# RWKV-7 recurrence: two 128-column products per chunk and head in place of four of 64 columns, y and its group norm by tokens

## The chip, the cores and the metric

The kernel runs on one core of a Trainium2 chip. The metric is the device time of one execution in microseconds (us), as the median of several runs. The profile is one execution taken by the hardware profiler; its times are counted from the first instruction.

## The reference, cut to what matters

The program is a two-layer encoder trunk over 512 tokens and 2048 channels: an RWKV-7 layer, then differential attention, each with a post-norm. The change is in the first layer, which has 32 heads of 64 channels. Each head keeps a 64 x 64 state:

```
def step(S, inp):                     # per token, all heads
    r_t, w_t, k_t, v_t, kk_t, a_t = inp
    sa = S @ kk_t
    S = S * w_t - outer(sa, kk_t * a_t) + outer(v_t, k_t)
    y = S @ r_t
...
mu, var = mean(y), var(y)             # per head and token
y = (y - mu) * rsqrt(var + GN_EPS) * gn_g + gn_b
y = y + sum(r * k * r_k) * v          # the bonus
out = (y * silu(g)) @ w_out
```

## The kernel before, in words

**Dense products.** Every projection is a run of 16 products, each with 16 k-tiles. For a k-tile, `step` issues three 128x512 matmuls into the tile `mm` (operands are split in a high and a low part). After each k-tile `fill.tick()` lets every pending job, a Python generator, issue its next piece; a job's `yield n` makes it sit out n ticks. Matmuls and DMAs keep the order in which the program issues them, on TensorE and on the queue of SP. The other engines' instructions are ordered by a scheduler, and those under `tc.high_priority()` go early.

**The recurrence by chunks.** Tokens are cut in 8 chunks of 64 (`NCH`, `L`), heads are taken in 16 pairs, a pair to 128 partitions. While the value projection runs (and the first gate products), these jobs share the ticks:

- `phase2(p)` prepares pair p: products of the keys `bdK` with `AR` (128 columns, two per tick), the centred values by tokens (`cen`, products of 64 columns into either half of the partitions, 16 instructions per tick), transposes of `bdK` (four per tick), products of the inverses `bdX` with `R`. The results are kept in `LAR`, `W` and `Q` (`qs` in the profile). It takes some 12 ticks of the 16 that a pair has.
- `chain(p)` runs the recurrence of pair p, two ticks per chunk. In the first tick one product per head, `LAR` with the state in `W`, gives u (tile `u`), which ScalarE copies into `W` (L829, L830). In the second tick one product per head, `Q` with `W`, gives the new state, which VectorE scales, adds to `nl` and writes to `W` (L844), for all chunks but the last; then two products per head add y in the tile `y`, one bank for the pair. All of these have 64 weight columns: head 0 writes partitions 0 to 63, head 1 partitions 64 to 127.
- `post(p)` makes the group norm with channels on partitions: squares, two 128x512 products with ones (`onesr`) for the sums, an inverse root by Newton steps on 128x512 tiles, gain and bonus, then one DMA to `d_y`.
- `solve` and `join` make the triangular inverses of a group of four pairs on GpSimd, with small products (64 weight columns) by `join`.

An F32 product is two instructions in the trace (a weight load and a matmul each), a transpose or an F32R product one: 30 products `u` of a pair are 60 instructions, its 32 products `y` are 64.

**Around it.** `load_r`, `load_k`, `load_ar` and `load_x` bring a pair's data from DRAM on SP's queue, `gates()` loads `d_y` later, multiplies it by the gate and splits it for the output projection. The inputs `xin` of the next projection are loaded by GpSimd's queue and mixed by ScalarE and GpSimd. Between these jobs there is no other order than the ticks.

## Time and profile before

| what | value |
|---|---|
| median of 3 runs | 2375.23 us (2374.12 to 2375.89) |
| span of the profiled execution | 2371.4 us |
| its own time beside the span | not given by the page; the median lies 3.8 us above the span |
| TensorE busy | 2281.1 us, 96% of the span |
| VectorE, ScalarE, GpSimd busy | 1371.7, 1085.0, 598.1 us |
| mean granted TensorE clock | 0.983 |

The span is from the first to the last instruction; the runs are timed from outside. Busy times are sums over an engine's instructions, and as matmuls overlap, a busy TensorE is not one at its peak: how long it takes for a piece of work is read from the starts.

### The profile page before, as it was taken

The page shows a single profiled execution, that of the slowest core. Times are in us where ns is not written, and L with a number is a line of the kernel's source. Part 1 is how long each engine was busy: PE and PEld are TensorE (multiplying, and loading weights), DVE is VectorE, ACT ScalarE, POOL GpSimd, SP SyncE. Part 2 cuts the span into 40 slices and gives each one's busy share as a digit, 9 for nine tenths or more (in the row PEclk, how much of TensorE's full clock was granted, in tenths as well). Part 3 has the DMA queues.
Part 4 walks back from the last instruction along what each step waited for, and adds up shares of the span by engine and source line. Part 5 has one row for each costly group of instructions (what it writes and reads, how often), then busy time and mean ns, then how long its engine had stood idle before and what let it go on. Part 6 is the DMA issues. An engine that isn't in the chain of part 4 may idle for free.

```text
span 2371.4 us, 34536 instructions
## 1 busy us (share of the span) xinstructions
PE 2281.1 (96%) x12894; PEld 1822.3 (77%) x12894; DVE 1371.7 (58%) x2451; ACT 1085.0 (46%) x2228; POOL 598.1 (25%) x817
## 2 busy tenths in 40 slices
PE   8999999989999999999999989999999999999995
PEld 5887877777667776678888768888888888888884
DVE  7556887795566666764445465353453544536554
ACT  6556655564555556643333353343333433334223
POOL 4223052858563335720023240000000000000113
PEclk9999999989999999999999999999999999999997
DMA  6445555577546545533333312222222222222222
GB/s 213 143 136 178 169 190 177 170 222 213 135 126 162 150 132 146 153 102 135 116 107 120 116 62 89 89 80 89 89 81 96 80 91 81 89 89 80 98 90 88
DMA packets 195079, 294.93 MB, mean 124 GB/s; under 512 B 115296, under 2 KB 119648, under 8 KB 194912
## 3 DMA queue, kind: packets, MB, share of 16 engines
q10 hardware_dynamic: 45648, 166.22, 20.8%
q1 hardware_dynamic: 144144, 109.71, 16.3%
q0 software_dynamic: 5120, 16.81, 2.5%
q8 instruction: 101, 1.65, 0.3%
q14 instruction: 66, 0.54, 0.1%
HBM read 239.13 MB, written 45.15 MB: 120 GB/s over the span
## 4 chain that ended last, share of the span: by engine, by line
PE 79%; POOL 7%; DVE 4%; issue 3%; DMA 3%; ACT 2%; SPq 1%; POOLq 0%; ACTq 0%; DVEq 0%
PE mm L105 64%; PE big L105 6%; PE u L105 2%; POOL z L605 2%; POOL tm L603 2%; DMA xin<-in_xT 2%; PE s L105 1%; PE y L105 1%; PE o L105 1%; PE big L108 1%; POOL xm L269 1%; SPq L111 1%; PE t L108 1%; POOL xin L268 1%; DVE wlo L176 1%
## 5 line engine op out<-in xcount | busy, mean ns | idle before, releaser
L105 PE MATMUL mm<-xh,whi 128*128 128x512 f32 x2560 | 1043.6, 408 | 6.7 <-ACT xh L231 2.3
L105 PE MATMUL mm<-xl,whi 128*128 128x512 f32 x2560 | 1006.7, 393 | 11.5 <-DVE xl L232 6.6
L105 PE MATMUL mm<-xh,wlo 128*128 128x512 f32 x2560 | 1006.3, 393 | 5.7 <-DVE wlo L176 5.5
L176 DVE TENSOR_TENSOR wlo<-wraw,whi 128x512 fp32r<-128x512 f32 x640 | 474.5, 742 | 597.7 <-ACT whi L175 564.3
L175 ACT CAST whi<-wraw 128x512 fp32r<-128x512 f32 x640 | 396.9, 620 | 727.3 <-PE mm L105 712.7
L105 PEld LDWEIGHTS mm<-xh,wlo 128*128 128x128 f32 x2560 | 483.9, 189 | 112.3 <-DVE wlo L176 8.5
L105 PEld LDWEIGHTS mm<-xl,whi 128*128 128x128 f32 x2560 | 485.4, 190 | 105.2 <-DVE xl L232 10.6
L105 PEld LDWEIGHTS mm<-xh,whi 128*128 128x128 f32 x2560 | 484.7, 189 | 104.6 <-ACT xh L287 4.9
L1118 POOL TENSOR_SCALAR dist<-dist 128x512 f32<-128x512 f32 x8 | 12.4, 1546 | 654.6 <-DVE zz L1148 654.6
L836 POOL TENSOR_SCALAR nl<-W,gls 64x64 f32<-64x64 f32 x224 | 115.0, 513 | 158.6 <-DVE W L844 146.3
L844 DVE SCALAR_TENSOR_TENSOR W<-u,gls,nl 64x64 f32<-64x64 f32 x224 | 63.4, 283 | 91.8 <-PE u L105 70.5
L266 ACT ACTIVATE xm<-xin,omu 128x512 f32<-128x512 f32 x96 | 68.2, 721 | 46.3 <-DMA xin<-in_xT 36.8
L603 POOL TENSOR_TENSOR tm<-z,at 128x31 f32<-128x31 f32 (+15 forms) x124 | 81.1, 654 | 31.1 <-DMA at<-d_ad 22.8
L605 POOL TENSOR_TENSOR z<-z,tm 128x31 f32<-128x31 f32 (+15 forms) x124 | 85.9, 693 | 8.4
L969 POOL TENSOR_TENSOR lna<-lna,zt 128x512 f32<-128x512 f32 x26 | 42.6, 1639 | 170.0 <-DVE zt L1244 115.8
L268 POOL TENSOR_SCALAR xin<-xin,vec 128x512 f32<-128x512 f32 x54 | 48.7, 902 | 140.6 <-ACT xm L266 52.1
L269 POOL TENSOR_TENSOR xm<-xm,xin 128x512 f32<-128x512 f32 x54 | 81.8, 1517 | 3.5
L829 ACT COPY W<-u 64x64 f32<-64x64 f32 x128 | 26.3, 205 | 101.6 <-PE u L105 94.7
L105 PEld LDWEIGHTS u<-W,LAR 128*64 128x64 f32 x512 | 28.7, 135 | 55.5 <-DVE W L844 27.3
L1077 POOL TENSOR_TENSOR xin<-xin,lns 128x512 f32<-128x512 f32 x15 | 19.7, 1311 | 194.6 <-ACT lns L957 148.9
L1147 ACT ACTIVATE sc<-sc,mx 128x128 f32<-128x128 f32 (+3 forms) x64 | 35.9, 561 | 57.8 <-DVE mx L1145 57.8
L288 DVE TENSOR_TENSOR xl<-xm,xh 128x512 fp32r<-128x512 f32 x64 | 57.4, 909 | 6.4 <-ACT xh L287 5.6
(246 smaller groups left out, 2742.2 us busy)
## 6 DMA issues: line engine op xcount, KB each, us to landing
wraw<-in_w_in ACTq DMA_DIRECT2D x125, 512.0 KB, 3.7
wraw<-in_w_oa ACTq DMA_DIRECT2D x32, 512.0 KB, 3.6
wraw<-in_w_v ACTq DMA_DIRECT2D x32, 512.0 KB, 3.5
wraw<-in_w_k ACTq DMA_DIRECT2D x32, 512.0 KB, 3.4
wraw<-in_w_q ACTq DMA_DIRECT2D x32, 512.0 KB, 3.5
wraw<-in_w_g ACTq DMA_DIRECT2D x32, 512.0 KB, 3.5
wraw<-in_w_ob ACTq DMA_DIRECT2D x32, 512.0 KB, 3.5
xin<-in_xT POOLq DMA_DIRECT2D x48, 256.5 KB, 3.8
```

The lines of the kernel that those rows point to most:

```text
L105: tc.keep_in_program_order(nc.tensor.matmul(*args, **kw))
L108: tc.keep_in_program_order(nc.tensor.transpose(*args))
L175: S.copy(hi, raw)
L176: V.tensor_sub(lo, raw, hi.bitcast(F32))
L266: S.mul(t, xt[:, 1:T + 1], sc)
L268: G.tensor_scalar(xp, xp, mu, 0.0, ALU.mult, ALU.add)
L269: G.tensor_add(t, t, xp)
L288: V.tensor_sub(lo, raw, hi.bitcast(F32))
L603: G.tensor_tensor(tv, z[:, j:j + 1, 0:n].broadcast_to([P, ni, n]), at_[:, j, j + 1:H2].rearrange("p (i o) -> p i o", o=1).broadcast_to([P, ...
L605: G.tensor_tensor(z[:, j + 1:H2, 0:n], z[:, j + 1:H2, 0:n], tv, ALU.subtract)
L836: G.tensor_scalar(nl[r], W[r, h, c, 0], gl[r], 0.0, ALU.mult, ALU.add)
L844: V.scalar_tensor_tensor(W[r, h, c + 1, 0], pm_[r, 0:L], gl[r], nl[r], ALU.mult, ALU.add)
```

## The change

In `chain`, the weights of a product become the whole of `LAR[:, h, c]` (128 columns: the 64 for u and the 64 for y) and of `Q[:, h, c]` (64 for the state, 64 for y), and the moving operand stays a block of 64 columns of `W`. So each chunk and head has two products with 128 weight columns, and y comes out by tokens, in two parts in the half that u and the state do not use. ScalarE copies u and the first part of y together, VectorE adds the second part once per two chunks. The last chunk, too, has its product with `Q`. One PSUM tile holds two chunks; the bank of `y` goes to a third `u` buffer.

`post` works with tokens on partitions: the sum of squares is a reduction along the free axis, the inverse root is made on 128x8 values, then four transposes bring y back to channels. Four DMAs with runs of 256 bytes store `d_y`. Gain and bonus move to `gates()`; for this the bonus is stored in `d_b` by `phase2` and loaded again. `AR` is kept by chunks, and `LAR` is loaded by three DMAs, two with runs of 256 bytes. Comments are taken out, so lines move; the diff is cut to what works differently.

```diff
-    d_ar = dtiles("d_ar", [P, 2, T])
+    d_ar = dtiles("d_ar", [P, NCH, 2, L])
...
-        LAR = p2.tile([P, 2, 2, NCH, L], F32, tag="LAR", name="LAR")
-        W = p2.tile([P, 2, NCH, 2, L], F32, tag="W", name="W")
-        for h, r in HEADS:
-            dma(LAR[r, h], AR[r].rearrange("p w (c t) -> p w c t", t=L))
+        LAR = p2.tile([P, 2, NCH, 2, L], F32, tag="LAR", name="LAR")
+        W = p2.tile([P, NCH, 5, L], F32, tag="W", name="W")
+        dma(LAR[lo_, 0], AR[lo_])
+        for w in range(2):
+            dma(LAR[hi_, 1, :, 1 - w], AR[hi_, :, w])
...
-            S.mul(Q[hi_, 1, cq], pxv[hi_], -1.0)
+            S.mul(Q[hi_, 1, cq, L:P], pxv[hi_, :, 0:L], -1.0)
+            S.mul(Q[hi_, 1, cq, 0:L], pxv[hi_, :, L:P], -1.0)
...
-        bv = p2.tile([P, T], F32, tag="bv", name="bv")
+        bv = p2.tile([P, T], F32, tag="bv", name="bv", bufs=1)
         V.tensor_mul(bv, vt, st["bz"])
...
+        dma(d_b[p], bv)
...
     def chain(p):
...
         for c in range(NCH):
-            pu = ps_u.tile([P, T], F32, tag="u", name="u")
+            cc = c % 2
+            if cc == 0:
+                pc = ps_u.tile([P, T], F32, tag="u", name="u").rearrange("p (c k h t) -> p c k h t", k=2, h=2, t=L)
             for h, r in HEADS:
-                mm(pu[r, 0:L], lhsT=LAR[:, h, 0, c], rhs=W[:, h, c, 0], start=True, stop=True)
+                mm(pc[:, cc, 0, h], lhsT=LAR[:, h, c].rearrange("p w t -> p (w t)"), rhs=W[:, c, 4 * h], start=True, stop=True)
             with tc.high_priority():
-                S.copy(W[lo_, 0, c, 1], pu[lo_, 0:L])
-                S.copy(W[hi_, 1, c, 1], pu[hi_, 0:L])
+                for h, r in HEADS:
+                    S.copy(W[r, c, 1 + h:3 + h], pc[r, cc, 0])
...
             yield 1
+            for h, r in HEADS:
+                mm(pc[:, cc, 1, h], lhsT=Q[:, h, c], rhs=W[:, c, 1 + 2 * h], start=True, stop=True)
             if c + 1 < NCH:
-                pm_ = ps_u.tile([P, T], F32, tag="u", name="u")
-                for h, r in HEADS:
-                    mm(pm_[r, 0:L], lhsT=Q[:, h, c, 0:L], rhs=W[:, h, c, 1], start=True, stop=True)
                 with tc.high_priority():
                     for h, r in HEADS:
-                        V.scalar_tensor_tensor(W[r, h, c + 1, 0], pm_[r, 0:L], gl[r], nl[r], ALU.mult, ALU.add)
-            for h, r in HEADS:
-                mm(py[r, cs], lhsT=W[:, h, c, 0], rhs=LAR[:, h, 1, c], start=True, stop=False)
-                mm(py[r, cs], lhsT=W[:, h, c, 1], rhs=Q[:, h, c, L:P], start=False, stop=True)
+                        V.scalar_tensor_tensor(W[r, c + 1, 4 * h], pc[r, cc, 1, h], gl[r], nl[r], ALU.mult, ALU.add)
+            if cc:
+                for h, r in ((0, hi_), (1, lo_)):
+                    V.tensor_add(ys[r, c - 1:c + 1], W[r, c - 1:c + 1, 2], pc[r, :, 1, h])
             yield 1
-        ys = p2.tile([P, T], F32, tag="ys", name="ys", bufs=1)
-        S.copy(ys, py)
...
     def post(p):
-        hi = p2.tile([P, T], F32R, tag="ngy", name="hi", bufs=1)
-        lo = p2.tile([P, T], F32R, tag="ngu", name="lo", bufs=1)
-        S.copy(hi, y2)
-        V.tensor_sub(lo, y2, hi.bitcast(F32))
-        yield 3
-        pv = big()
-        mm(pv, lhsT=onesr, rhs=hi, start=True, stop=False)
-        mm(pv, lhsT=onesr, rhs=lo, start=False, stop=True)
-        V.tensor_scalar(y2, pv, 1.0 / L, GN_EPS, ALU.mult, ALU.add)
-        rs = rsqrt(y2, p2, [P, T], "ng", 1, True)
-        V.scalar_tensor_tensor(ys, ys, RS_C, rs, ALU.mult, ALU.mult)
-        V.scalar_tensor_tensor(bv, ys, vcol("gg", p), bv, ALU.mult, ALU.add)
-        yield 10
-        dma(d_y[p], bv)
+        S.activation(y2, ys, AF.Square)
+        ss = p2.tile([P, NCH], F32, tag="ss", name="ss")
+        V.tensor_reduce(ss, y2, axis=AX.X, op=ALU.add)
+        V.tensor_scalar(ss, ss, 1.0 / L, GN_EPS, ALU.mult, ALU.add)
+        rs = rsqrt(ss, p2, [P, NCH], "ng")
+        V.tensor_mul(ys, ys, rs.rearrange("p (c o) -> p c o", o=1).broadcast_to([P, NCH, L]))
+        yield 9
+        pt = big()
+        for i in range(4):
+            transpose(pt[:, i * P:(i + 1) * P], ys[:, 2 * i:2 * i + 2].rearrange("p c v -> p (c v)"), ident)
+        yt = p2.tile([P, 4, 2, L], F32, tag="yt", name="yt", bufs=1)
+        S.copy(yt, pt.rearrange("p (i h t) -> p i h t", h=2, t=L))
+        yield 2
+        for cc, r in HEADS:
+            for h in range(2):
+                dst = d_y[p][h * L:(h + 1) * L].rearrange("v (i c t) -> v i c t", c=2, t=L)
+                dma(dst[:, :, cc], yt[r, :, 1 - h])
...
     def gates():
...
             dma(y, d_y[p])
+            dma(bb, d_b[p])
             yield 6
+            V.scalar_tensor_tensor(y, y, der[:, 4, p:p + 1], bb, ALU.mult, ALU.add)
             V.scalar_tensor_tensor(y, y, vcol("gb", p), th, ALU.add, ALU.mult)
```

## Rows read from the trace of the kernel before

**Rows 1.** The page, its first part: busy time of each engine.
```profile
PE 2281.1 (96%) x12894; PEld 1822.3 (77%) x12894; DVE 1371.7 (58%) x2451; ACT 1085.0 (46%) x2228; POOL 598.1 (25%) x817
```
**Rows 2.** Busy time by stretches of the recurrence: length, engines (instructions), clock, DMA, GB/s.
```profile
575.00:660.00 85.00, 81.14 (x752) 58.58 (x748) 40.95 (x88) 41.69 (x103) 52.10 (x101) 0.98 0.64 163
660.00:915.00 255.00, 253.45 (x2502) 181.25 (x2501) 158.66 (x338) 143.97 (x366) 96.83 (x196) 1.00 0.54 143
915.00:990.00 75.00, 66.25 (x561) 46.16 (x560) 59.27 (x100) 50.19 (x117) 60.43 (x81) 0.98 0.56 150
990.00:1042.00 52.00, 52.00 (x458) 35.09 (x457) 37.09 (x77) 29.41 (x75) 21.59 (x33) 1.00 0.27 83
```
**Rows 3.** Chain of waits, 747 to 762 us: start, us, what.
```profile
747.67 0.59 PE big L108 x4
748.26 0.69 PE mm L105 x3
748.95 0.27 PE u L105 x4
749.22 0.28 PE y L105 x8
749.50 0.89 PE mm L105 x3
...
755.53 0.64 PE big L105 x4
...
760.37 0.27 PE u L105 x4
760.63 0.89 PE mm L105 x3
```
**Rows 4.** Chain of waits, ticks of `cen` and of a last chunk.
```profile
771.24 0.47 PE big L105 x16
771.71 0.89 PE mm L105 x3
...
773.14 1.25 PE big L105 x18
...
993.66 0.39 PE y L105 x8
```
**Rows 5.** Chain of waits in the key projection: `bd` x `AR` (x8), transposes (x4).
```profile
276.14 0.89 PE big L105 x8
...
277.73 0.44 PE big L108 x4
```
**Rows 6.** Timeline of TensorE, products with `hsel` in the key projection.
```profile
255.90 0.95 PE L105 MATMUL big<-cst,sq 128*128 128x2 f32 x8
256.71 0.48 PE L105 MATMUL mm<-xh,whi 128*128 128x512 f32 x1
257.02 0.39 PE L105 MATMUL mm<-xl,whi 128*128 128x512 f32 x1
```
**Rows 7.** Timeline of one chunk whose `u` products start at 747.34 and 748.88.
```profile
747.34 0.34 PE L105 MATMUL u<-W,LAR 128*64 128x64 f32 x4
747.74 0.21 ACT L829 COPY W<-u 64x64 f32<-64x64 f32 x1 [0.48 <-PE u L105]
748.30 0.37 ACT L784 COPY qs<-big 64x256 f32<-64x256 f32 x1
748.88 0.34 PE L105 MATMUL u<-W,qs 128*64 128x64 f32 x4
749.36 0.60 DVE L844 SCALAR_TENSOR_TENSOR W<-u,gls,nl 64x64 f32<-64x64 f32 x2 [1.46 <-PE u L105]
```
**Rows 8.** Waits of the weight loads, 720 to 900 us: us, times, longest.
```profile
PEld u L105 <- issue: 18.7, 51, 0.4
```
**Rows 9.** The page, costliest groups: the split of weights on VectorE (busy us, mean ns).
```profile
L176 DVE TENSOR_TENSOR wlo<-wraw,whi 128x512 fp32r<-128x512 f32 x640 | 474.5, 742 | 597.7 <-ACT whi L175 564.3
```
**Rows 10.** DMA queues, 600 to 1050 us: packets, MB, share of 16 engines.
```profile
q1 hardware_dynamic: 66496, 39.33, 35.5%
```

More of the change, by code (lines that the diff above doesn't have):

```diff
@@ L304, in dtiles @@
         return [dtile(f"{name}{p}", shape) for p in range(NPAIR)]
-    d_r, d_y = (dtiles(n, [P, T]) for n in ("d_r", "d_y"))
-    d_ar = dtiles("d_ar", [P, 2, T])
+    d_r, d_y, d_b = (dtiles(n, [P, T]) for n in ("d_r", "d_y", "d_b"))
+    d_ar = dtiles("d_ar", [P, NCH, 2, L])
     d_kz = dtiles("d_kz", [P, 2 * T + NCH])
@@ L433, in trunk @@
     V.tensor_scalar(omu, vec[:, 0:6], -1.0, 1.0, ALU.mult, ALU.add)
-    der = const.tile([P, 4, NT], F32, name="der")
+    der = const.tile([P, 5, NT], F32, name="der")
     V.tensor_scalar_mul(der[:, 0], vec[:, VECS.index("w0")], 0.5)
@@ L505, in decay @@
         S.activation(kp, ta, AF.Identity, scale=der[:, 2, p:p + 1], bias=der[:, 3, p:p + 1])
-        AR = p1.tile([P, 2, T], F32, tag="AR1", name="AR1", bufs=2)
-        V.tensor_mul(ch(AR[:, 1]), ch(rt), gx[:, :, 1:L + 1])
+        AR = p1.tile([P, NCH, 2, L], F32, tag="AR1", name="AR1", bufs=2)
+        V.tensor_mul(AR[:, :, 1], ch(rt), gx[:, :, 1:L + 1])
         kz = p1.tile([P, 2 * T + NCH], F32, tag="kz", name="kz", bufs=2)
@@ L692, in open_p2 @@
             G.memset(fixed[i], 0.0)
-    ps_u = ps_y = None
+    ps_u = None
     def load_r(p):
@@ L707, in load_ar @@
     def load_ar(p):
-        AR = p2.tile([P, 2, T], F32, tag="AR", name="AR", bufs=1)
+        AR = p2.tile([P, NCH, 2, L], F32, tag="AR", name="AR", bufs=1)
         dma(AR, d_ar[p])
@@ L761, in phase2 @@
                 for w, msk in ((0, m_lt), (1, m_le)):
-                    V.tensor_tensor(LAR[r, h, w, cq], pkv[r, :, w], over(msk[r], [L, 4, L]), ALU.mult)
+                    V.tensor_tensor(LAR[r, h, cq, w ^ h], pkv[r, :, w], over(msk[r], [L, 4, L]), ALU.mult)
             yield 1
@@ L784, in phase2 @@
             S.copy(Q[hi_, 0, cq, 0:L], ptv[hi_, :, 0:L])
-            S.copy(Q[lo_, 1, cq, 0:L], ptv[lo_, :, L:P])
+            S.copy(Q[lo_, 1, cq, L:P], ptv[lo_, :, L:P])
             yield 2
@@ L848, in chain @@
+            if cc:
+                for h, r in ((0, hi_), (1, lo_)):
+                    V.tensor_add(ys[r, c - 1:c + 1], W[r, c - 1:c + 1, 2], pc[r, :, 1, h])
             yield 1
-        ys = p2.tile([P, T], F32, tag="ys", name="ys", bufs=1)
-        S.copy(ys, py)
         st["ys"] = ys
-        y2 = p2.tile([P, T], F32, tag="y2", name="y2", bufs=1)
-        S.activation(y2, py, AF.Square)
-        st["y2"] = y2
         done.add(("chain", p))
     def post(p):
-        st = sts.pop(p)
-        ys, y2, bv = st["ys"], st["y2"], st["bv"]
@@ L872, in post @@
-        V.scalar_tensor_tensor(bv, ys, vcol("gg", p), bv, ALU.mult, ALU.add)
-        yield 10
-        dma(d_y[p], bv)
+        ys = sts.pop(p)["ys"]
+        y2 = p2.tile([P, NCH, L], F32, tag="yt", name="y2", bufs=1)
+        S.activation(y2, ys, AF.Square)
[4 more added lines that the diff above has]
+        V.tensor_mul(ys, ys, rs.rearrange("p (c o) -> p c o", o=1).broadcast_to([P, NCH, L]))
@@ L906, in gates @@
             th = ths.pop(p)
-            y = pg.tile([P, T], F32, tag="yl", name="yl")
+            y = py.tile([P, T], F32, tag="yl", name="yl")
+            bb = py.tile([P, T], F32, tag="bb", name="bb")
             dma(y, d_y[p])
+            dma(bb, d_b[p])
             yield 6
+            V.scalar_tensor_tensor(y, y, der[:, 4, p:p + 1], bb, ALU.mult, ALU.add)
             V.scalar_tensor_tensor(y, y, vcol("gb", p), th, ALU.add, ALU.mult)
@@ L920, in begin_g @@
     def begin_g(p):
-        nonlocal xb
+        nonlocal xb, py
         if p == GL:
@@ L927, in begin_g @@
             xb = ctx.enter_context(tc.tile_pool(name="xb", bufs=NT, reuse_waits="tile"))
+            py = ctxG.enter_context(tc.tile_pool(name="py", bufs=2, reuse_waits="tile"))
             done.add("xb")
```

30 lines of the change are left out of this document (14 added, 16 removed).

## The prediction

> **What bounds the kernel now.** I read the page first: TensorE is busy 96% of the span, every other engine 58% or less [rows 1]. That is an average, so next I cut the recurrence (575 to 1042 us) into stretches. From 660 to 915 us TensorE is busy 253.45 of 255 us and from 990 to 1042 all of 52; VectorE has 158.66 of 255, ScalarE 143.97. From 575 to 660 it misses 3.9 us and from 915 to 990, where the next projection's inputs arrive, 8.8 [rows 2]. The chain of waits inside the first of the full stretches is TensorE's own instructions, without a gap [rows 3]. So there the order of instructions on TensorE is the clock: what a tick costs on TensorE is what it costs the kernel. A pair has 16 ticks.
>
> To price the change I need a tick's extra over its three dense matmuls. With nothing foreign ahead of them these take 0.69 us, and 0.89 after a `u` or `y` group [rows 3]. A visit of the four `u` instructions therefore costs 0.27 + 0.20 = 0.47; `u` and the eight of `y` cost 0.27 + 0.28 + 0.20 = 0.75. Eight more instructions for 0.28: **0.035 us for one with 64 weight columns, and a fixed 0.33 for each visit.** The weight loads' waits show a part of it: before `u` they stand up to 0.4 us without a releaser, 51 times [rows 8].
>
> Full-width F32 groups look different: `bd` x `AR`, eight instructions of 128 weight and 128 moving columns, cost 0.89, four transposes 0.44 [rows 5]. Eight with 128 weight and 2 moving columns take 0.81 until the next dense matmul starts, and that one 0.31 where a third of 0.69 is usual: 0.89 again [rows 6]. So the number of moving columns from 2 to 128 does not matter, and the new products, 128 by 64, lie between two equal rows: **0.101 an instruction and 0.08 fixed for a visit.** This is the choice on which the sum hangs. The lower bound would be half of it, if 64 moving columns cost half of 128; I do not take it, since 2 columns cost as much as 128. The upper bound is 0.11 without a fixed part.
>
> **The ticks of a pair, before and after.** A visit of four new instructions costs 4 x 0.101 + 0.08 = 0.485 alone; behind another full group it adds 0.405, its fixed part being paid. One bare first tick goes from 0.47 to 0.485, +0.015. Two bare second ticks go from 0.75 to 0.485, -0.53 together. Two first ticks with four transposes go from 0.27 + 0.59 = 0.86 to 0.36 + 0.485, -0.03. Four first ticks with four 128-wide products go from 0.27 + 0.64 = 0.91 to 0.89, -0.08. Four second ticks with these go from 0.27 + 0.28 + 0.64 = 1.19 to 0.89, -1.20 [rows 3, 5]. The first tick with the 16 `cen` instructions (64 columns) costs 0.27 + 0.47 + 0.20 = 0.94; now `cen` pays the fixed part by itself, 0.94 - 4 x 0.035 = 0.80, and 0.405 comes on top: 1.20, +0.26. The second with `cen` and the two products with ones goes from 0.55 + 1.25 = 1.80 to 1.20, -0.60, the ones being gone. The last chunk, `y` alone, goes from 0.39 + 0.20 = 0.59 to 0.485, -0.10 [rows 3, 4]. The four transposes of `post` add 0.40, between 0.36 and 0.44 [rows 5].
>
> The sum is -1.87 us a pair, -29.9 for 16. The small products of `join`, 64 columns wide, share their fixed part with `u` today and won't afterwards: two ticks in about half of the pairs, some 0.1 each, 2 us. That leaves -28.
>
> **What of it reaches the end.** In the two full stretches, 307 of 467 us, all of it. In the other two TensorE waits for transfers and GpSimd, so I take half, by the same mixture of busy and waiting that the rows show [rows 2]. The factor is (307 + 80) / 467 = 0.83, and the gain 23 us.
>
> **New waits.** A shorter tick must still hold the turn from product to copy to product. A bare tick becomes 0.69 + 0.485 = 1.17. First tick: the copy starts 0.40 after `u` does [rows 7]. Now each copy needs both heads, so all four instructions at 0.101 apiece: 0.2 later, at 0.60. A copy of 64 columns takes 0.21 and one of 256 0.37 [rows 7]; I take 0.26 for 128. They end at 0.86 and 1.13, and head 0 is due at 1.17, head 1 at 1.37. Second tick: VectorE starts 0.48 after the product, two operations in 0.60 [rows 7]; head 1's now starts some 0.25 later and ends near 1.15, with 1.37 due. Both fit with 0.2 to 0.3 to spare if the engine is free. VectorE is busy 62% and ScalarE 56% of the full stretch [rows 2], with instructions near 0.7 us, as the commonest one, 742 ns [rows 9]: by an estimate 0.62 x (0.7 - 0.25)^2 / (2 x 0.7) = 0.09 a bare tick, some 0.3 a pair, 4 us in all. What queues behind a late copy on TensorE is the next product and, in order, the dense matmuls after it. Ticks with foreign work have 0.4 us more and take no share.
>
> **Costed at nothing.** VectorE loses the ten 128x512 operations of the norm and gets a reduction, nine narrow ones, one wide multiplication and eight additions of 64x128; ScalarE loses five wide copies and squares and gets two wide ones, two more halves in `Q` and longer copies. Both get less work in all, and the cover is TensorE's dense stream. The GpSimd `nl` work stays. In `gates()` one VectorE operation and one load per pair are added beside dense matmuls; without that cover the operation would cost about 0.7 us [rows 9] once, at the last tile. On SP's queue `post` now has four stores that wait for one ScalarE copy, ahead of the later loads of the next pairs, instead of one store that waits for the end of the norm; `phase2` has one more load and one more store. A pair's loads are issued a pair ahead, so nothing is late next, as long as the queue flows (third rival).
>
> Sum: -23 + 4 = -19. The profiled span is 2371.4, so 2352; the median stands 3.8 above it, and **the forecast is 2356 us**, with 2346 to 2366 for this case: the factor may be 0.6 to 1, the waits 0 to 8 us.
>
> **Beside a rule.** The rows give 0.101 us for a full weight load, whatever moves [rows 5, 6]. The Trainium skill, "TensorE: Matmul & The Clock Gate", section "LDWEIGHTS", puts a load at its columns over 1.2, so 107 ns for 128; by it the 64 instructions would cost an estimated 0.4 us a pair more, and the gain would be 18 us in place of 23. The rows decide.
>
> **Rivals.** *Narrow products were the cheap ones (slower).* If the fixed 0.33 stayed with the visit whatever its width, only the instructions would count: a chunk has 16 at 0.035 = 0.56 today and 8 at 0.101 = 0.81 afterwards, +0.25, for 128 chunks +32 us, 2407. It decides if a full visit costs over 0.25 fixed; 0.08 in two kinds of rows speaks against [rows 5, 6]. This would be the rule of the Trainium skill, "TensorEngine Tiling (Array Packing)", section "When to Use Tiling", which recommends column tiling for 64 weight columns, up to twofold; the same page, section "Key Properties", says that a change of the tiling drains the array, which agrees with the fixed part. Chance 0.05.
>
> *The turn becomes the clock (slower or same).* If the copies or VectorE's operations came 0.5 us late on each of four bare ticks of a pair, the 1.87 would be gone; that is the point from which it decides. At 0.7 us late it is +0.9 a pair, +15 us, 2390. For it: copies need both heads, and the margin is 0.2. Against: today's bare first tick, 0.69 + 0.47 = 1.16, is as short, and its chain shows no gap [rows 3]. Chance 0.14.
>
> *Short runs fill the queues (smaller gain).* `LAR` and `d_y` add 2048 runs of 256 bytes a pair. SP's queue now carries 66496 packets in 450 us, about 4100 a pair, for 35.5% of the engines' time [rows 10]; half as many again makes some 53%. If that delays inputs and weights where TensorE already waits, the 160 us of those stretches gain nothing and lose some 8 us: -28 x 0.66 + 4 + 8 = -6, about 2368. Chance 0.14.
>
> *Moving columns are the price (faster).* At 0.055 an instruction a pair gains 2.9 us more, until the turn binds; about 2325. Chance 0.05, as the rows with 2 columns exclude it nearly.
>
> **How the numbers follow.** The forecast has 0.62. A change within 0.2%, some 4.7 us, can hardly be told from none. Faster takes the forecast, the last rival and most of the packets': 0.78. Same takes the rest of these and a mild case of the turn: 0.10. Slower: 0.12. The range reaches from halfway to the cheap price, 2338, to where the turn eats the gain, 2378; it leaves out the two price rivals and the worse turn, some 0.16.
>
> **What would show it.** Right: a bare second tick's extra falls from 0.75 to about 0.49, eight full instructions in a row take 0.8, the weight loads' 0.4 us before `u` vanish, and the full stretch has a pair in some 25.8 us instead of 27.7. Wrong: `u` rows of TensorE with waits for ScalarE's `W` copies or VectorE's updates, 0.055 or 0.14 an instruction in the new groups, or longer waits for `xin` between 915 and 990 us.

## Result and the profile after

The changed kernel takes 2396.96 us (2396.14 to 2399.12, 4 runs), the kernel before in the same comparison 2374.68 (2370.57 to 2375.89, 4 runs): a ratio of 1.0095, 95% interval 1.0081 to 1.0110. It is 22 us slower where 19 us faster was forecast, and outside the range. One of e8's six runs below took 10056 us; e8's median and ratio are of the other five.

The page, first part, answers to [rows 1]. TensorE has 928 instructions less and 5.8 us less work, and the span is 24 us longer:
```profile
PE 2275.3 (95%) x11966; PEld 1875.0 (78%) x11966; DVE 1342.4 (56%) x2612; ACT 1071.3 (45%) x2212; POOL 575.5 (24%) x817
```
By stretches, as in [rows 2] (length, busy time of PE, PEld, DVE, ACT, POOL with instructions, clock, DMA share, GB/s):
```profile
575.00:660.00 85.00, 76.32 (x577) 64.56 (x577) 41.50 (x111) 40.16 (x102) 51.99 (x103) 0.96 0.66 162
660.00:915.00 255.00, 237.33 (x1840) 202.74 (x1838) 127.48 (x390) 126.48 (x335) 81.45 (x183) 0.97 0.54 137
915.00:990.00 75.00, 66.03 (x471) 54.10 (x469) 47.79 (x122) 47.11 (x110) 46.24 (x72) 0.98 0.69 183
990.00:1042.00 52.00, 47.06 (x324) 39.06 (x324) 31.35 (x83) 30.95 (x77) 22.40 (x41) 0.93 0.42 114
```
The stretch that was full, 660 to 915, now misses 17.7 us of TensorE, and its clock is 0.97 where it was 1.00. VectorE and ScalarE have less to do than before, as forecast, and that is no help. What TensorE waits for in that stretch (us, times, longest):
```profile
PE big L105 <- DMA bdK<-d_kz: 11.8, 6, 4.5
PE big L105 <- ACT W L779: 2.7, 6, 0.6
PE u L105 <- DVE W L851: 2.4, 3, 1.5
```
Most of it is a load, `bdK`, that was never late before. SP's queue, in the order in which it issues, shows why. Before, then after:
```profile
723.60 1.30 SPq L111 DMA_DIRECT2D bdK<-d_kz  x2
730.47 0.33 SPq L111 DMA_DIRECT2D d_y<-bv  x1
735.45 1.13 SPq L111 DMA_DIRECT2D LAR<-AR  x2
```
```profile
718.82 0.45 SPq L111 DMA_DIRECT2D R<-d_rb  x1
730.31 2.53 SPq L111 DMA_DIRECT2D d_y<-yt  x4
732.94 0.55 SPq L111 DMA_DIRECT2D AR<-d_ar  x1
733.58 1.29 SPq L111 DMA_DIRECT2D bdK<-d_kz  x2
734.96 0.73 SPq L111 DMA_DIRECT2D d_b<-bv  x1
```
After `R` at 718.82 the queue issues nothing for 11 us: the store of y stands next in line and waits for `yt`, which ScalarE finishes at 730.3. `AR` and `bdK` stand behind it. The one buffer of `bdK` was free from 726.2 on, when its last transposes ended. With the store moved behind the loads (e1) `bdK` is issued at 725.25.

A wait costs more than its length. Windows round the longest one, 4.47 us before the product at 799.47 (same columns), and that product in TensorE's timeline:
```profile
789.00:795.00 6.00, 5.95 (x38) 4.94 (x37) 2.06 (x6) 3.74 (x11) 1.59 (x4) 1.00 0.84 194
795.00:799.50 4.50, 0.03 (x1) 0.06 (x1) 3.49 (x12) 0.73 (x3) 1.47 (x4) 0.89 0.61 184
799.50:803.00 3.50, 3.50 (x13) 3.21 (x14) 0.09 (x1) 0.00 (x0) 0.00 (x0) 0.50 0.92 191
803.00:806.00 3.00, 3.00 (x16) 2.71 (x15) 2.59 (x7) 0.38 (x2) 0.63 (x2) 0.61 0.81 172
```
```profile
799.47 1.20 PE L105 MATMUL big<-AR,bdK 128*128 128x128 f32 x4 [4.47 <-DMA bdK<-d_kz]
```
After the wait the granted clock is 0.50, the lower of its two levels (1.2 of 2.4 GHz), and soon after it is back; from 806 to 812 it is 1.00. 3.5 us at 0.50 and 3.0 at 0.61 are 3.5 x 0.50 + 3.0 x 0.39 = 2.9 us of lost work: by this estimate the 4.5 us wait costs 7.4.

The instructions cost in sum what was forecast. The chain of waits where nothing is late, as in [rows 3]:
```profile
722.61 0.39 PE u L105 x4
723.00 0.44 PE big L108 x4
723.44 0.69 PE mm L105 x3
724.13 0.39 PE u L105 x4
724.52 0.75 PE mm L105 x3
```
A visit of four with four transposes takes 0.39 + 0.44 = 0.83 where 0.36 + 0.485 = 0.85 was forecast, and one alone 0.39 + 0.06 = 0.45 where 0.485 was. The weight loads show the price by itself: in the four `u` products from 743.68 on and the four of `bdK` behind them, loads start at 743.68, .79, .90, 744.02, .13, .24, .35 and .46, 0.11 us apart, whether 64 or 128 columns move.

**Two tables for what follows,** both worked out from TensorE's timelines, each of one execution. The first cuts the recurrence at the first `u` product of each pair (us; in pairs 0 to 3 GpSimd makes inverses, in 11 to 13 the gates' inputs):

| kernel | pairs 0 to 3 | 4 to 10 | 11 to 13 | 14 |
|---|---|---|---|---|
| before | 118.9 | 191.6 | 94.7 | 26.4 |
| after | 120.9 | 207.8 | 99.8 | 25.9 |
| e1 | 120.1 | 196.6 | 104.7 | 25.7 |
| e2 | 121.2 | 214.3 | 107.1 | 27.1 |
| e5 | 122.4 | 200.0 | 95.8 | 26.0 |
| e6 | 120.8 | 204.2 | 104.2 | 26.8 |
| e7 | 124.1 | 200.9 | 104.7 | 25.6 |
| e8 | 121.8 | 183.9 | 94.2 | 25.0 |
| e9 | 123.7 | 194.2 | 99.4 | 26.0 |
| e13 | 124.4 | 204.0 | 104.1 | 28.1 |
| e15 | 120.7 | 193.4 | 98.7 | 25.7 |
| e17 | 118.5 | 191.0 | 95.8 | 25.4 |
| e18 | 119.3 | 190.5 | 99.2 | 25.2 |

The second has the median length of a tick between 700 and 905 us, from the start of its first product to that of the next tick's, by what stands before its three dense matmuls (a tick thus holds the wait of the product that follows it); forecast is the prediction's extra plus the 0.69 us of these:

| ahead of the dense matmuls | before | forecast | after | e8 | e9 | e18 |
|---|---|---|---|---|---|---|
| second product alone | 1.44 | 1.17 | 1.24 | 1.25 | 1.24 | 1.25 |
| first product alone | 1.16 | 1.17 | 1.35 | 1.35 | 1.35 | 1.35 |
| second + `R` x `bdX` | 1.89 | 1.58 | 1.59 | 1.59 | 1.69 | 1.68 |
| second + `AR` x `bdK` | 1.89 | 1.58 | 1.61 | 1.59 | 1.59 | 1.59 |
| first + `R` x `bdX` | 1.60 | 1.58 | 1.59 | 1.69 | 1.80 | 1.79 |
| first + `cen` | 1.62 | 1.89 | 2.10 | 1.90 | 2.10 | 1.90 |
| second + `cen` | 2.48 | 1.89 | 2.37 | 2.01 | 2.37 | 1.90 |
| first + `R` x `bdX` + transposes of y | | 1.98 | 2.13 | | 2.13 | 2.13 |

The shortest second tick alone is 1.14 in each of the changed kernels: that is the price, and what the medians have above it is time lost to waits.

### The profile page after: what moved, and what is told of

Its sections match the earlier page's. It is cut to its first block, busy times and chain, and to the rows that moved or that the text cites. A ratio compares the mean times of both kernels' runs of the same rounds, so it can differ in the third digit from the quotient of the medians.

```text
span 2395.5 us, 32995 instructions
## 1 busy us (share of the span) xinstructions
PE 2275.3 (95%) x11966; PEld 1875.0 (78%) x11966; DVE 1342.4 (56%) x2612; ACT 1071.3 (45%) x2212; POOL 575.5 (24%) x817
## 3 DMA queue, kind: packets, MB, share of 16 engines
q1 hardware_dynamic: 179472, 118.10, 17.7%
## 4 chain that ended last, share of the span: by engine, by line
PE 72%; POOL 7%; DMA 7%; DVE 6%; issue 3%; ACT 2%; SPq 1%; POOLq 0%; ACTq 0%; DVEq 0%
PE mm L105 60%; PE big L105 4%; PE u L105 3%; POOL z L606 3%; POOL tm L604 2%; DMA xin<-in_xT 2%; PE s L105 1%; SPq L111 1%; DMA bdK<-d_kz 1%; PE o L105 1%; PE big L108 1%; DMA AR<-d_ar 1%; DVE wlo L176 1%; DMA bb<-d_b 1%; DMA at<-d_ad 1%
## 5 line engine op out<-in xcount | busy, mean ns | idle before, releaser
L844 POOL TENSOR_SCALAR nl<-W,gls 64x64 f32<-64x64 f32 x224 | 96.9, 432 | 194.8 <-DVE W L851 183.3
L839 ACT COPY W<-u 64x128 f32<-64x128 f32 x256 | 66.5, 260 | 130.4 <-PE u L105 126.7
L105 PEld LDWEIGHTS u<-W,LAR 128*128 128x128 f32 x512 | 75.7, 194 | 38.6 <-DVE W L851 30.1
L105 PEld LDWEIGHTS u<-W,qs 128*128 128x128 f32 x512 | 76.2, 196 | 27.2 <-ACT W L839 18.6
L105 PE MATMUL u<-W,LAR 128*128 128x64 f32 x512 | 79.2, 276 | 13.8 <-DVE W L851 13.0
L105 PE MATMUL u<-W,qs 128*128 128x64 f32 x512 | 77.1, 274 | 6.9 <-ACT W L839 6.4
```

What stands on the lines that cost most here:

```text
L105: tc.keep_in_program_order(nc.tensor.matmul(*args, **kw))
L839: S.copy(W[r, c, 1 + h:3 + h], pc[r, cc, 0])
L844: G.tensor_scalar(nl[r], W[r, c, 4 * h], gl[r], 0.0, ALU.mult, ALU.add)
```

## The experiments

Theories: A, the order on SP's queue; A2, the chain's steps stand on VectorE or ScalarE, which take their work in a fixed order, behind a foreign instruction that waits for something late; B, short runs fill the queues; C, a shorter tick no longer holds the turn from product to copy to product. Every ratio is to the kernel before, run beside it, with its 95% interval.

**e1 to e4: the store of y.** e1 moves it behind the loads of `AR` and `bdK`; e2 makes the kernel before do the opposite; e3 stores long runs (y lands in the wrong places of `d_y`); e4 takes the store to another queue.
```diff
--- after, post
+++ e1
-        yield 2
+        yield 5
         for cc, r in HEADS:
--- before, post
+++ e2
-        yield 10
+        yield 7
--- after, post
+++ e3
-        for cc, r in HEADS:
-            for h in range(2):
-                dst = d_y[p][h * L:(h + 1) * L].rearrange("v (i c t) -> v i c t", c=2, t=L)
-                dma(dst[:, :, cc], yt[r, :, 1 - h])
+        dma(d_y[p], yt.rearrange("p i h t -> p (i h t)"))
--- after, post
+++ e4
-                dma(dst[:, :, cc], yt[r, :, 1 - h])
+                tc.keep_in_program_order(S.dma_start(dst[:, :, cc], yt[r, :, 1 - h]))
```


> The changed kernel, the four stores of y issued three ticks later (yield 5 in place of 2), behind the next pair's loads of AR and bdK on SP's queue. Theory A, the queue's order: the loads no longer wait for the store, TensorE's waits for bdK (about 12 us from 660 to 900) go, a pair takes about 26 us, total 2350 to 2368. Theory B, short runs fill the queues: the runs are as many and as short, total within 5 us of 2397. Theory C, the turn from product to copy to product is the clock: 2390 or more.

> The kernel before, its one store of y issued three ticks earlier (yield 7 in place of 10), ahead of the next pair's loads of AR and bdK, nothing else changed. Theory A: the queue waits for the end of the norm, bdK is issued some 7 us later than before while its slack was about 8, so 0 to 12 us slower, 2375 to 2387, with SP's waits for the store doubled and the landing of bdK later. Theories B and C: no change, 2375 within 3.

> The changed kernel with one store of y in runs of 2 KB at the same place in the queue in place of four in runs of 256 bytes; y reaches memory in the wrong places. Theory A: the queue still waits for y, only some 2 us of issuing a pair are saved, so 2380 to 2395. Theory B: half of the short runs and three issues are gone, half of the loss comes back and more, 2360 to 2378. Theory C: 2390 or more.

> The changed kernel with the four stores of y, at the same tick, issued by ScalarE's queue behind its own copy. Theory A: SP's queue is free, 2350 to 2370, perhaps some us back for the four issues on ScalarE. Theory B: the runs are as many, 2390 to 2400. Theory C: 2390 or more.

Measured: e1 2391.61, ratio 1.0080 (1.0065 to 1.0095); e2 2410.23, 1.0165 (1.0144 to 1.0187); e3 2388.59, 1.0070 (1.0053 to 1.0086); e4 2395.52, 1.0099 (1.0081 to 1.0117). e2 is the clearest: three ticks' difference in the place of one store makes the kernel before 38 us slower, where theory A had said 0 to 12, and its waits from 660 to 915 are those of after:
```profile
PE big L105 <- DMA bdK<-d_kz: 14.3, 7, 3.1
```
In e1 the waits for `bdK` are gone and pairs 4 to 10 take 196.6 us instead of 207.8; but pairs 11 to 13 take 104.7 instead of 99.8, and some 5 us arrive, where theory A had said 29 or more; the intervals of e1 and after overlap. What is next in line stands in e1's timeline:
```profile
741.97 0.69 DVE L808 TENSOR_TENSOR bv<-vt,bz 128x512 f32<-128x512 f32 x1 [2.14 <-DMA bz<-d_kz]
742.66 0.59 DVE L851 SCALAR_TENSOR_TENSOR W<-u,gls,nl 64x64 f32<-64x64 f32 x2
743.31 0.81 PE L105 MATMUL u<-W,LAR 128*128 128x64 f32 x4 [2.13 <-DVE W L851]
```
VectorE stands still with `bv`, which waits for `bz`, and the chain's update stands behind it. So A holds and is not enough. In e4 SP's queue is free of the store, and ScalarE pays: its chain copies stand behind the four issues, which take 2.5 us a pair there, and three of them 9.9 us more until a store has landed; TensorE waits 17.0 us in 17 for these copies between 600 and 1050 us, after 6.4 in 8.

**e5 and e9: VectorE's order.** e5 is e1 with `bz` loaded a pair ahead, the squares `y2` in a free part of `W`, and one buffer in the norm's root; e9 also writes `bv` over `bz`.
```diff
--- e1, load_k and post
+++ e5
+        bz = p2.tile([P, T], F32, tag="bz", name="bz", bufs=2)
+        dma(bz, d_kz[p][:, T:2 * T])
+        bzs[p] = bz
...
-        y2 = p2.tile([P, NCH, L], F32, tag="yt", name="y2", bufs=1)
+        ys, y2 = st["ys"], st["W"][:, :, 0]
...
-        rs = rsqrt(ss, p2, [P, NCH], "ng")
+        rs = rsqrt(ss, p2, [P, NCH], "ng", bufs=1)
--- e5, phase2
+++ e9
-        bv = p2.tile([P, T], F32, tag="bv", name="bv", bufs=1)
-        V.tensor_mul(bv, vt, bzs.pop(p))
+        bv = bzs.pop(p)
+        V.tensor_mul(bv, vt, bv)
```


> The changed kernel with the store of y behind the loads of AR and bdK (as in e1_store_later), and two more edits: bz gets two buffers and is loaded with bdK of its pair, a pair earlier than before, so that the product bv on VectorE needn't wait for it; the squares y2 go into a part of W that is free by then, so that ScalarE's square needn't wait until the store of the last yt has landed. Theory A2 (VectorE and ScalarE take their work in a fixed order, and an instruction that waits for a late transfer holds up the chain's state update behind it; TensorE then waits and its clock falls): TensorE's waits for the state update, 17.5 us in 15 in e1, fall to 8 to 10 us, as in before, its half clock goes with them, and the time falls from 2392 to 2365-2380. Theory B (short runs fill the queues): nothing is moved off the queues, 2386-2394. Theory C (the turn product, copy, product, state update is too long for a tick): nothing of the turn is shorter, 2388-2394.

> e5_bz_a_pair_ahead with one edit more: the product bv is written over bz, which has two buffers, so that VectorE needn't wait until the last bv has been stored. In e5's trace TensorE's longest wait (4.3 us at 767.6, for the state update) is this one: VectorE waited 5.6 us with bv for the store of the last, and the state update stood behind it. Theory A2 (the state update stands, in an engine's fixed order, behind a foreign instruction that waits for something late): pair 5's 33.7 us fall to 27-28, pairs 7 and 8 lose 0.5 to 1 each, and the time falls from 2387 by 6 to 10, to 2377-2381. Theory C (the turn is too long in every tick): no change over 2 us, 2385-2389.

Measured: e5 2387.08, 1.0060 (1.0043 to 1.0076), a gain, but less than the 2365 to 2380 of A2. The reason stands in its timeline of VectorE and TensorE:
```profile
766.34 0.69 DVE L809 TENSOR_TENSOR bv<-vt,bz 128x512 f32<-128x512 f32 x1 [5.58 <-DMA d_b<-bv]
766.95 0.59 DVE L852 SCALAR_TENSOR_TENSOR W<-u,gls,nl 64x64 f32<-64x64 f32 x2
767.59 1.12 PE L105 MATMUL u<-W,LAR 128*128 128x64 f32 x4 [4.29 <-DVE W L852]
```
`bv` no longer waits for `bz`; it waits for the store of the last `bv`, as it has one buffer. e9 takes that wait away: 2382.40, 1.0038 (1.0024 to 1.0052), and pair 5 falls from 33.7 us to 27.1, as expected; by the ratios the time falls by 5 us, not 6 to 10. A2 is shown for `bv`: one instruction, two late things, one behind the other.

`bv` still waits in e9, for `bz` again. VectorE comes to it right behind the load, and the chain's update stands behind it:
```profile
727.45 0.61 SPq L111 DMA_DIRECT2D bz<-d_kz  x1
730.89 0.69 DVE L809 TENSOR_TENSOR bz<-vt,bz 128x512 f32<-128x512 f32 x1 [3.00 <-DMA bz<-d_kz]
731.62 0.60 DVE L852 SCALAR_TENSOR_TENSOR W<-u,gls,nl 64x64 f32<-64x64 f32 x2
```
It waits so in every pair from here to 900 us, 3.0 to 3.6 us each, and in e17 and e18 too. TensorE loses 0.1 to 0.4 us a pair by it in e9: the tick in which `bv` stands takes 1.68 to 2.03 us, where the price is 1.59.

**e6 and e7: short runs.** e6 is e1 without short runs in the recurrence, e7 is e5 with the same edits. The four transfers of y with short runs move to the gates' load.
```diff
--- e1, phase2, phase1 and post
+++ e6
-        for w in range(2):
-            dma(LAR[hi_, 1, :, 1 - w], AR[hi_, :, w])
+        dma(LAR[hi_, 1], AR[hi_])
...
-        dma(d_ar[p], AR)
+        dma(d_ar[p][lo_], AR[lo_])
+        for w in range(2):
+            dma(d_ar[p][hi_, :, 1 - w], AR[hi_, :, w])
...
-                dma(dst[:, :, cc], yt[r, :, 1 - h])
+        dma(d_y[p], yt.rearrange("p i h t -> p (i h t)"))
```


> The changed kernel with the store of y behind the loads of AR and bdK, and no 256-byte runs in the recurrence: yt is stored in one transfer of long runs, and the four transfers with short runs are in the gates' load of y, after the recurrence; AR's second half is stored with its two parts swapped (two transfers of short runs in the key stage), so that LAR's second half is loaded in one transfer of long runs. Results are the same. Theory B: the queue's packets in 600 to 1050 fall from 95132 to some 65000, as before the change, loads land earlier, and the time falls from 2392 to 2365-2380. Theory A2: the loads' order on the queue is left as it is, bz still stands behind LAR, 2382-2391 (the long store alone gave 8 us). Theory C: 2388-2394.

> The edits of e5_bz_a_pair_ahead and e6_long_runs together. If A2 and B are the whole cause, the chain's forecast saving of some 20 us is now to be seen: 2350-2365, faster than before (2372). If the one of them is the cause, the time is that of the better one of the two within 3 us. Theory C: 2380 or more in all three.

Measured: e6 2409.18, 1.0158 (1.0142 to 1.0173); e7 2406.66, 1.0143 (1.0124 to 1.0161). The packets of e6 in 600 to 1050 us fell to 68368, nearly those of [rows 10], and the kernel is slower than e1. B falls as a cause: without short runs pairs 4 to 10 take 204.2 us in e6 (e1 196.6) and 200.9 in e7 (e5 200.0). In e6 VectorE waits for `bz` in most of pairs 4 to 11, and the gates, which now load with short runs, lose some 3 us more than e1's (from the last `cen` product to the first product `st<-cst,lna` 354.6 us, e1 351.3, after 347.8). In e7 the gates lose 6 us against e5's, and pairs 11 to 13 take 104.7 us for 95.8; what they wait for was not followed up. e3, 6 us below after by the ratios, has one issue of 0.3 us at the head of the queue where after has four in 2.5.

**e8: the chain without the norm.** e8 is e7 without squares, sums, root, scaling and transposes of y.
```diff
--- e7, post
+++ e8
-        S.activation(y2, ys, AF.Square)
...
-        dma(d_y[p], yt.rearrange("p i h t -> p (i h t)"))
+        dma(d_y[p], ys.rearrange("p c v -> p (c v)"))
```


> As e7_both, with the group norm by tokens and its transposes left out: ys is stored as the chain leaves it, in one transfer, where yt would be stored (squares, sums, root, scaling, four transposes and a copy for each pair are left out). Sixteen pairs lose four transposes (some 0.45 us each pair on TensorE) and a wait of a visit, 7 to 9 us in all, if that is all the norm costs: 2343-2358 where e7_both is 2350-2365. A norm that holds up the chain on VectorE or ScalarE: 15 us or more below e7_both. Theory C: still 2375 or more, since the chain is the same.

Measured: 2379.83, 1.0038 (1.0025 to 1.0050), by the ratios 25 us below e7, three times what the norm's TensorE instructions are worth. Not all of it is the norm's: 8.6 us are one wait of e7, for the store of `bv` in pair 5 (34.0 us, e8 25.4), and 10.5 lie in pairs 11 to 13. The closer comparison is e9. Pairs 4 to 10 take 26.3 us each in e8, before 27.4, e9 27.7, and of these 1.4 us the transposes are some 0.4; the second tick with `R` x `bdX` and the first with `cen` come at their forecast length, the second with `cen` within 0.12. So the norm's work on ScalarE and VectorE costs the chain more than its transposes do. What C expected, "still 2375 or more", is met too.

**e10 to e12: later is not better.** e10 is e9 with the inverse's late steps three ticks later, e11 with `xin` issued on SP's queue too, e12 gives both to the kernel before.
```diff
--- e9, solve and join
+++ e10
+        yield 3
         zt = inv.tile([P, H2, H2], F32, tag="at", name="zt")
...
-        yield 5
+        yield 3
...
-            yield 6
+            yield 9
             diagonal(bda, a21)
--- e10 and before, x_tile
+++ e11 and e12
-        (dma if first else dma_x)(xt, xT[m])
+        (dma if first or sp else dma_x)(xt, xT[m])
```


> e9_bv_in_place with the inverse's two late steps put later in the order: the transposed copy zt on VectorE three ticks later (it waited for GpSimd's z, 1.8 us before the wait of 2.2 us at 685.2 in e5), and GpSimd's placing of the blocks bda and bdx three ticks later after their loads (they waited for the load of wv, and the nl of the state update stood behind them). Theory A2: the waits in pairs 0 to 3, 10.7 us in e5 with some 5 us of lower clock behind them, fall by half: 5 to 9 us below e9, 2369-2375. Theory C: within 2 us of e9. If the later steps make a pair's inverse late, its loads wait and it is slower than e9; then TensorE's waits are for bdX or R and not for the state update.

> e10_late_work_later with the loads of xin for the gates' inputs issued on SP's queue in place of GpSimd's, where they stand behind nl and the mixing. In e5 ScalarE waits for xin 14.5 us in 8 (before: 8.9 in 3), and the chain's copy behind it holds TensorE 6 us in pair 12. Theory A2: the waits of pairs 11 to 13, 12 us in e5, fall by half or more: 5 to 10 us below e10, 2360-2369, faster than before (2372). Rival: SP's queue is in order too, and its loads now wait for the mixing, so the waits only move (bdK, AR, LAR late): e10 or slower.

> The kernel before with the last two edits (zt and the placing of the blocks three ticks later, xin for the gates on SP's queue). It misses some 13 us of TensorE's time in pairs 1, 2 and 11 to 13 as well. If these edits relieve work that both kernels share, this one gains 3 to 8 us, 2364-2369, and the changed kernel's own saving is what e11 has beyond that. If before's order had no use for them, 2370-2374.

Measured: 2422.50, 1.0206 (1.0183 to 1.0230); 2415.22, 1.0178 (1.0163 to 1.0193); 2403.52, 1.0119 (1.0101 to 1.0138). A miss for all three: `join` runs once a pair, so three ticks there push the last pairs out past the projection that covers them. The first `th` of the gates, at 1014.3 in e9, comes 52 us later in e10, and TensorE has only 133 instructions in the 36 us ahead of it:
```profile
1030.00:1066.00 36.00, 29.18 (x133) 21.59 (x134) 24.42 (x59) 19.14 (x41) 23.64 (x32) 0.91 0.34 95
```
The expectation named a late load as the risk; what came was a chain without cover. The kernel before suffers in the same way (first `th` at 1056.7), so this says nothing of the change.

**e13 to e16: turn against single waits,** each from e9. e13 copies the second head on VectorE, e14 puts only `zt` two ticks later, e15 only `xin` on SP's queue, e16 is all three.
```diff
--- e9, chain
+++ e13
-                for h, r in HEADS:
-                    S.copy(W[r, c, 1 + h:3 + h], pc[r, cc, 0])
+                S.copy(W[lo_, c, 1:3], pc[lo_, cc, 0])
+                V.tensor_copy(W[hi_, c, 2:4], pc[hi_, cc, 0])
--- e9, solve
+++ e14
+        yield 2
         zt = inv.tile([P, H2, H2], F32, tag="at", name="zt")
...
-        yield 5
+        yield 3
```


> e9_bv_in_place with the copy of the second head's first product on VectorE, beside the first head's on ScalarE, in place of two on ScalarE one after the other. Theory C (the turn: product, two copies of 0.26 us in a row, product): the second copy ends some 0.25 us sooner, the ticks with the second product alone fall from 1.24 to 1.17 us, the second one with cen from 2.37 to some 2.1, a calm pair from 27.0-28.8 to 26.3-28.0, and the time falls by 8 to 14, to 2368-2374. Theory A2 alone: calm pairs stay within 0.2 us, the waits for xin are halved in pair 12 for one head only, 2379-2384. Against it: VectorE has 16 more instructions a pair, and a head's copy may come late there.

> e9_bv_in_place with the transposed copy zt on VectorE two ticks later, and the inverse's stores at the same tick as before. Unlike e10 nothing of the later steps is moved. Theory A2: the waits at 593.0 (2.5 us) and 684.0 (2.1 us) go, with the lower clock behind them: pairs 0 and 3 fall from 28.7 and 32.4 to 27 and 29, 3 to 7 us in all, 2375-2379. Theory C: within 2 us of e9.

> e9_bv_in_place with the loads of xin for the gates' inputs on SP's queue, and nothing else (in e11 it stood together with the later joins, which moved the last pairs past the projection). Theory A2: ScalarE's waits for xin in pairs 11 to 13 fall from 14 us to under 8, pair 12 from 38.0 to 33, 4 to 8 us, 2374-2378. Rival: the wait is on the loads' buffer or landing and not on the issue, then pair 12 stays at 36 to 39 and the time within 3 us of e9.

> e13, e14 and e15 together. If turn and single waits are the whole of what is left, their gains add: 2358-2368, faster than the kernel before (2373). If one only moves another's wait, it is no better than the best one of the three.

Measured: e13 2406.16, 1.0135 (1.0114 to 1.0156); e14 2380.94, 1.0030 (1.0021 to 1.0039); e15 2378.99, 1.0029 (1.0018 to 1.0040); e16 2406.99, 1.0144 (1.0125 to 1.0164). ScalarE's waits from 900 to 1040 us in e9 and in e15:
```profile
ACT xm L266 <- DMA xin<-in_xT: 12.6, 5, 5.9
```
```profile
ACT xm L266 <- DMA xin<-in_xT: 5.9, 5, 2.4
```
They halve, and the time gains 3.4 us, just short of the 4 to 8. e14 gains 1.5 us, less than its 3 to 7. The intervals of both overlap with e9's, so neither gain is clear of noise. In e14's trace `zt` still stands before the update in pair 3. e13 is worse by 24 us, and its timeline shows where:
```profile
810.91 0.66 PE L105 MATMUL u<-W,qs 128*128 128x64 f32 x4 [1.05 <-DVE W L840]
```
The copy is shorter in line on ScalarE but comes behind VectorE's other work, and TensorE waits about 1 us in every pair behind the first half of `cen` (that tick 3.25 us, e9 2.10). The second one with `cen` falls to 2.00, so ScalarE's copies do hold that one up. The tick with the second product alone stays at 1.24, and the one with the first goes from 1.35 to 1.42: the copies side by side help neither. e16 has e13's wait again (10.7 us in 18 between 700 and 905) and tells nothing more.

**e17 and e18: the norm off the chain's engines.** e17 is e14 and e15 with the squares and the scaling of `ys` on GpSimd; e18 also writes the products with `cen` to two PSUM tiles.
```diff
--- e9 with the edits of e14 and e15, post
+++ e17
-        S.activation(y2, ys, AF.Square)
+        G.tensor_tensor(y2, ys, ys, ALU.mult)
...
-        V.tensor_mul(ys, ys, rs.rearrange("p (c o) -> p c o", o=1).broadcast_to([P, NCH, L]))
+        G.tensor_tensor(ys, ys, rs.rearrange("p (c o) -> p c o", o=1).broadcast_to([P, NCH, L]), ALU.mult)
--- e17, phase2
+++ e18
-        pt = big()
         for c in range(NCH):
+            if c % 4 == 0:
+                pt = big()
```


> e14 and e15 together (zt two ticks later, xin on SP's queue), with two of the norm's wide instructions moved: the squares from ScalarE and the scaling of ys from VectorE to GpSimd, which is busy 7 of 27 us in a calm pair. If the norm's work on ScalarE and VectorE is what the turn waits for (e9's calm pairs 27.75 us, 26.3 without the norm, 0.4 of it the transposes), calm pairs fall by 0.4 to 1.0 and the time to 2362-2372, at or under the kernel before. If the turn is its own length, calm pairs stay at 27.5-27.9 and the time is that of e14 and e15 added, 2375-2379. Against it: nl stands on GpSimd behind the two new instructions, over 1 us each; where that decides, TensorE's waits for the state update grow and it is slower than 2379.

> e17_norm_on_gpsimd with the products with cen written to two PSUM tiles, one for each four chunks, so that the second four needn't wait for the copies of the first (TensorE waits some 0.4 us a pair there, and the second tick with cen takes 2.37 us in e9, 2.0 where ScalarE is free). If that wait is for the tile: 0.3 to 0.4 us a pair, 5 to 6 us below e17. If ScalarE is simply late with all its copies, the next transposes wait for the tile instead: within 2 us of e17.

Measured: e17 2374.85, 1.0005 (0.9996 to 1.0014), the time of the kernel before; e18 2367.75, 0.9971 (0.9961 to 0.9981), 5.6 us under it and 29 under the changed kernel. e17 stands 3 us under e14 and e15 added (no run has these two alone), which is within the noise, and over the 2362 to 2372 expected. Its pairs 4 to 10 fall to 27.3 us, at the low end of the 0.4 to 1.0 expected; so the norm's place is at most a part of the turn's cost. e18 gains 7 more where 5 to 6 were expected, and that is clear of noise. The second tick with `cen` in TensorE's timeline, e9 and e18:
```profile
831.21 0.55 PE L105 MATMUL u<-W,qs 128*128 128x64 f32 x4
832.15 0.69 PE L105 MATMUL big<-cst,vt 128*64 128x64 f32 x16 [0.40 <-ACT W L780]
...
833.58 0.55 PE L105 MATMUL u<-W,LAR 128*128 128x64 f32 x4
```
```profile
825.41 0.55 PE L105 MATMUL u<-W,qs 128*128 128x64 f32 x4
825.89 0.69 PE L105 MATMUL big<-cst,vt 128*64 128x64 f32 x16
...
827.31 0.55 PE L105 MATMUL u<-W,LAR 128*128 128x64 f32 x4
```
2.37 us become 1.90, the forecast's 1.89. The chunks five to eight had waited until ScalarE was done copying chunks one to four out of the same tile. In the kernel before, the eight `y` instructions of that tick ran meanwhile, and the second half of `cen` began as the copies ended:
```profile
772.41 0.58 ACT L776 COPY W<-big 64x512 f32<-64x512 f32 x1
772.81 0.34 PE L105 MATMUL y<-qs,W 128*64 128x64 f32 x4
773.04 0.69 PE L105 MATMUL big<-cst,vt 128*64 128x64 f32 x16
```
Whether `cen` in two tiles, or any of these edits alone, would help the kernel before was not tried, save for e12.

## Why the prediction was wrong

**The price held in sum.** 0.101 us a full instruction and 0.08 a visit, the choice on which the sum hung, gave 1.58 for a tick with eight of them, and the trace has 1.59. How it was divided was not right: the loads start 0.11 us apart and a visit has no fixed part, which is the upper bound that the prediction named. For eight the two agree (0.89), for four it is 0.45 and not 0.485, a little cheaper than forecast. Before, `u` stood behind weight loads that waited up to 0.4 us without a releaser [rows 8]; that row is gone after. Both price rivals fall: 0.11 is twice the 0.055 of the one, and the other needs a fixed part over 0.25. (Halfway to the cheap price, from 2356 to 2325, is 2340 and not 2338; nothing hangs on it.)

The rule on LDWEIGHTS in the Trainium skill, "TensorE: Matmul & The Clock Gate", section "LDWEIGHTS", gives 107 ns for 128 columns, by estimate 0.69 + 8 x 0.107 = 1.55 for that tick. The trace is a little over it and not under it; the 0.4 us a pair in "Beside a rule" came of putting the rule's price on top of the fixed 0.08.

**The step that failed first** is the one in "Costed at nothing": "A pair's loads are issued a pair ahead, so nothing is late next, as long as the queue flows". It named the four stores ahead of the later loads, and priced them at nothing. A store that waited stopped the queue for all that stood behind it: `AR` and `bdK` became late, and by e2 this order alone is worth 38 us in the kernel before. The price of a wait was also left out: behind the longest one the clock was at 0.50 for 3.5 us. Behind the queue stood VectorE's order: `bv` for `bz`, then for its own store. By the ratios, after to e15 took 0.66% off, some 16 us: the queue (e1, 0.15%), `bz` and `y2` (e5, 0.20%), `bv` (e9, 0.22%), `xin` (e15, 0.09%). The 0.57% from after to e9 are clear of noise; the first and the last step by themselves are not. From after to the forecast ratio of 0.992 it is 1.75%, so this step has somewhat over a third of the miss.

**The second is "New waits", in size.** It allowed 0.3 us a pair for the turn and forecast a pair in some 25.8 us. e9, in whose pairs 4 to 10 TensorE has no single wait over 0.6 us left, has 27.7 there, before 27.4: the 1.87 is wholly gone. The step checked the bare ticks, 0.2 to 0.3 to spare with engines free, and gave ticks with foreign work no share, since they have 0.4 more. The loss was in these: the second tick with `cen` is 0.48 over its forecast, the first 0.21, those with transposes or `R` x `bdX` 0.11 to 0.22; only then the bare ones, 0.07 and 0.18. VectorE and ScalarE do less work in sum, but what they do comes in front of a copy. The rival "the turn becomes the clock" had the effect right and its place wrong; it was given 0.14. e14 and e15 added stand at 1.0021; e17 and e18 take 0.50% off that, 12 us, by giving the turn room, 0.34% of it by `cen` in two tiles.

**What the bare ticks wait for** stands in e9's timelines. The first product alone, ScalarE's copies, the second product; then the second product alone, VectorE's update, the next first product:
```profile
708.25 0.55 PE L105 MATMUL u<-W,LAR 128*128 128x64 f32 x4
708.64 0.37 ACT L805 ACTIVATE qs<-big 64x256 f32<-64x256 f32 x1
709.02 0.53 ACT L840 COPY W<-u 64x128 f32<-64x128 f32 x2
709.60 0.66 PE L105 MATMUL u<-W,qs 128*128 128x64 f32 x4
```
```profile
754.61 0.55 PE L105 MATMUL u<-W,qs 128*128 128x64 f32 x4
755.29 0.60 DVE L852 SCALAR_TENSOR_TENSOR W<-u,gls,nl 64x64 f32<-64x64 f32 x2 [1.06 <-PE u L105]
755.95 0.66 PE L105 MATMUL u<-W,LAR 128*128 128x64 f32 x4
```
The sum under "New waits" gave each head its own due time, 1.17 and 1.37. Here head 0's product starts only when the copies or updates of both heads are done, at 1.35 and 1.34. All 59 second products of e9 between 700 and 905 us do so, and 35 of 52 first ones; in the tick at 751.85, which took 1.14, the first product went ahead with head 0 alone. VectorE had been idle for 1.06 us and took 0.60, so that second tick is the turn's own length and no late thing; the copies stood behind two of `qs`, at 0.77 and not at 0.60.

**What of it reaches the end.** In the two stretches with transfers and GpSimd work, half of the saving was to come through. None did: pairs 0 to 3 and 11 to 13 take 213.6 us before and 214.3 even in e17. In both kernels VectorE's update waits there for GpSimd's `nl` (589 to 710 us: before 11.9 us in 11, e17 9.8 in 5) and ScalarE for `xin` (905 to 1000 us: 8.9 in 3, 5.3 in 4). That a cheaper tick only waits sooner there fits this and is not shown by a run.

**The third rival,** short runs, falls by e6, and with it the sentence that it would be the queue's fullness that delays: with 95132 packets for 66496 the share rose from 35.5% [rows 10] to 40.1%, not 53.

Open: e18 is still 0.5%, 12 us, above the forecast ratio of 0.992. Its pairs 4 to 10 take 27.2 us where 25.8 was forecast; by the second table three ticks with the second product alone, one with the first, three with `R` x `bdX` and one with the transposes make some 1.0 of these 1.4. How much of it a `bv` that never waits, or a product per head that waits for its own copy alone, would give back was not tried. The rest lies in pairs 0 to 3 and 11 to 13. That the waits for `xin` and `z` are the whole of these was only argued, since e10 to e12 moved more than was meant.

## What to carry to other kernels

When a change takes work off the engine that sets the pace, list for each in-order queue and engine what stands behind every moved or new instruction that can wait, and treat "it waits" as "everything behind it waits"; fewer busy microseconds on the other engines say nothing of that. The operations that are removed were also cover: for each, ask which copy or load ran beneath it (here the `y` products, above the copies out of one PSUM tile). Price a wait of several microseconds on TensorE with the lower clock that follows it, and look in the trace for the next waiter before calling a fix done: here four came, one behind the other, and the third fix still left `bv` waiting. For a turn of product, copy and product, ask which copies the next product waits for in fact: a due time for each head was worth 0.2 us a tick on paper and nothing in the trace.
